# An order by hand for the first loads of a fused gated-convolution layer: SP's transfers and VectorE's instructions kept in plan order from the second to the twelfth pass

## Chip, cores and metric

One core of one Trainium2 chip. The metric is the time of one execution in microseconds (us). TensorE (PE in the profile) multiplies, VectorE (DVE) and ScalarE (ACT) do the elementwise work, GpSimd (POOL) a little of it, and SyncE (SP) issues nearly all transfers between HBM and the core's own memory, which 16 DMA engines carry out. Each engine works through its own instructions in a fixed order, and waits at an instruction whose inputs are not there yet.

## What is computed

One layer of a decoder trunk, for one sequence of 256 tokens with 2048 features, all in float32:

```python
h = rmsnorm(x, norm_g)
mod = einsum('bd,df->bf', silu(c), ada_w) + ada_b      # ada_w: 2048 x 6144
shift, scale, gate = split(mod, 3)
h = h * (1 + scale) + shift
b_gate, c_gate, v, g = split(h @ sc_w_in, 4)           # sc_w_in: 2048 x 16384
u = causal_depthwise_conv(c_gate * v, conv_w)          # width 3
y = (b_gate * u * silu(g)) @ sc_w_out                  # sc_w_out: 4096 x 2048
out = rmsnorm(x + gate * y, final_g)
```

## The kernel before

**Products.** Features lie on the 128 partitions, so the 2048 input features are 16 blocks k. A float32 product is made of three faster ones: a number is split into a high part (hi, a cast on ScalarE, line 356) and a low part (lo, the difference, on VectorE, line 361), and TensorE multiplies hi by hi, hi by lo and lo by hi (line 496). The tokens are split in the same way into hT. So each load of weights (raw_s, line 540) goes through three engines: SP's transfer, ScalarE's cast, VectorE's subtraction; then TensorE uses it. A load of 512 KB holds 8 blocks of 128 x 128, which are 24 matmuls of 256 columns.

**Why there are passes.** The block k of the tokens can only be used once shift and scale of these features are known, and these come from ada_w, 32 MB of which are read by the same DMA engines. The first two blocks are made ready in a written-out beginning. The other fourteen follow two at a time: a group of two blocks is read in eight pieces (`ada_piece`, line 454), each of two transfers of 256 KB (line 464) and two sums on VectorE (`ada_sums`, lines 476 and 478). After the eighth piece `ada_done` turns the sums on TensorE and finishes the two token blocks. Meanwhile TensorE works with the blocks that are there: the first 16 of 32 column tiles are 16 pairs (ch, q) of a chunk and a quarter, and a pass (`part`, line 522) multiplies one pair with the blocks k0 to k1. ScalarE or VectorE (`keep`, line 514) keeps the sum in acc for later passes.

**The plan.** `plan()` (line 52) simulates loads and engines with fixed costs and returns the order of passes and ada pieces. Its first steps, numbered from 0 (a pass is named with its blocks; n:m means k from n to m):

```
0 pass 0:2   1 pass 0:2   2 pass 0:2   3 ada 2   4 pass 0:2   5 ada 2   6 pass 0:2   7 pass 0:2
8 ada 2   9 pass 0:2   10 ada 2   11 pass 0:2   12 ada 2   13 pass 0:2   14 ada 2   15 pass 0:2
16 pass 0:2   17 ada 2   18 pass 0:2   19 ada 2   20 pass 0:2   21 ada 4   22 pass 0:4   23 ada 4
24 pass 0:4   25 ada 4   26 ada 4   27 pass 0:4   28 ada 4   ...
```

Step 0 is the first pass, whose weights the written-out beginning has loaded; steps 1, 2, 4, 6, 7, 9, 11, 13, 15, 16 and 18 are the second to the twelfth. Each loads 512 KB; step 22 is the first that loads 1024 KB. Steps 3 to 19 that say "ada 2" are the eight pieces for the blocks 2 and 3.

**Who sets the order on an engine.** The loop at line 575 traces the steps in plan order, but the framework's scheduler then orders each engine's instructions itself, by a priority (the order of tracing) and by when its own simulation has them ready. The kernel bends this in four ways: `in_order()` (line 166) chains all that is traced in it, engine by engine, and is used for the beginning (closed at line 434) and the end; `behind(last)` (line 179) puts instructions behind named ones of the same engine; `later(n)` (line 189) lowers the priority, and the ada sums are traced with `later(300)`; `tc.issue_after` does the same as `behind`. Such links cost no semaphore: they only fix an order. In `part`, high parts stand behind the copy that keeps an earlier pass (`kept`, line 545), and the low parts of the fourth and the fifth pass behind the last sum of the first and the second piece (`added`, line 547).

**Buffers.** raw, hi and lo have three tiles each, of 1024 KB. Two loads of 512 KB share one tile (`places`, line 369). Step 7's load goes to the tile that held the first pass's weights, step 11's to that of steps 1 and 2, step 22's to that of steps 11 and 13. The transfers of ada pieces have four tiles (at).

Of the kernel before, what the change touches and what calls it, by code (L numbers as in the profile page):

```python
# [51 lines left out]
def plan():  # L52

    steps, ready = [], [0.0] * ADA[0]
    done = {}
    pieces = [(sum(ADA[:g]), nk, i) for g, nk in enumerate(ADA) if g for i in range(4 * nk)]
    load, pe, dve, act = 0.0, 4.0, 0.0, 0.0  # L60
    burst = SLOT // P

    def ada():
        nonlocal load, dve
        k0, nk, i = pieces.pop(0)
        steps.append(("ada", k0, nk, i))
        load = max(load, dve - AAHEAD) + ALOAD
        dve = max(dve, load + 2.0) + VPIECE
        if i == 4 * nk - 1:
            ready.extend([dve + ALAG] * nk)  # L70

    def products(n, need):

        nonlocal load, pe, dve, act
        load = max(load, pe - WAHEAD)
        pe = max(pe, need, load + min(n, burst) * LOAD + WLAG) + n * PRODUCTS
        load += n * LOAD
        act = max(act, load + 2.0) + n * SBLOCK
        dve = max(dve, load + 2.0) + n * VBLOCK

    def fill():

        while pieces and max(load, dve - AAHEAD) + ALOAD + burst * LOAD + WLAG < pe:
            ada()

    order = [(ch, q) for ch in range(NCH) for q in QUARTERS]
    new = list(order)
    while new or any(k < KT for k in done.values()):
        fill()
        hi = sum(r <= pe for r in ready)  # L90
        if new:
            p = new.pop(0)
            done[p] = 0
        else:
            old = [p for p in order if done[p] < KT]
            p = old[0] if hi == KT else min(old, key=lambda p: done[p])
            while hi == done[p]:
                while len(ready) == hi:
                    ada()
                pe = max(pe, ready[hi])  # L100
                hi = sum(r <= pe for r in ready)
        products((hi - done[p]) * CT, ready[hi - 1])
        seed = done[p] > 0 and act < dve
        if done[p] == 0:
            act += SCOPY
        elif seed:
            act += SSEED
        else:
            dve += VSUM
        steps.append(("mm", *p, done[p], hi, seed))  # L110
        done[p] = hi
    while pieces:
        ada()
    return steps
# [3 lines left out]
def short_conv_layer(ctx: ExitStack, tc: tile.TileContext, x, c, norm_g, ada_w, ada_b, w_in, conv_w, w_out, final_g, out):  # L118
    nc = tc.nc
# [25 lines left out]
    def w_tile(kind, name, dtype=F32, i=None):  # L145

        if i is None:
            i = nth[kind] % 3
            nth[kind] += 1
        return wpool.tile([P, SLOT], dtype, tag=f"{kind}{i}", name=name, bufs=1)  # L150
# [12 lines left out]
    after = mybir.DependencyInfo(mybir.DependencyClass.NoSync, mybir.DependencyReason.DATA)  # L163

    @contextmanager
    def in_order():

        traced = nc.cur_bb.bb.instructions
        n = len(traced)
        yield  # L170
        last = {}
        for ins in list(traced[n:]):
            if ins.engine in last:
                tc.add_manual_dep(ins, last[ins.engine], after, reason="in order")
            last[ins.engine] = ins.name
        ended.update(last)

    @contextmanager
    def behind(last):

        traced = nc.cur_bb.bb.instructions
        n = len(traced)
        yield
        for ins in list(traced[n:]):
            if ins.engine in last:
                tc.add_manual_dep(ins, last[ins.engine], after, reason="behind")
# [13 lines left out]
    ended = {}  # L200
# [4 lines left out]
    def rows_tile(name):  # L205
        return const.tile([96, P], F32, tag="rows", name=name)
# [20 lines left out]
    for n, (j, kk) in enumerate(((0, 4), (4, 4), (8, 4), (12, 2), (14, 1), (15, 1))):  # L227
        at = w_tile(("lo", "hi")[n % 2], "at0")[:, : kk * 2 * NK0 * P]
        at = at.rearrange("p (k s f) -> p k s f", k=kk, s=2)
# [124 lines left out]
    def split_hi(raw, n, hi=None):  # L354
        hi = hi_tile() if hi is None else hi
        nc.scalar.copy(hi[:, :n], raw[:, :n])  # L356
        return hi

    def split_lo(raw, n, hi, lo_tag="lo", lo=None):
        lo = lo_tile(lo_tag) if lo is None else lo  # L360
        last_low[0] = nc.vector.tensor_tensor(  # L361
            out=lo[:, :n], in0=raw[:, :n], in1=hi[:, :n].bitcast(F32), op=ALU.subtract
        )
        return hi, lo
# [4 lines left out]
    def places(n):  # L369

        if n <= HALF and other_half[0]:
            tiles, other_half[0] = other_half[0], None
            return [b[:, HALF:SLOT] for b in tiles]
        tiles = raw_tile("raw_s"), hi_tile(), lo_tile()
        other_half[0] = tiles if n <= HALF else None
        return tiles
# [23 lines left out]
    for k in range(KT):  # L400
        c_k = silu_c[:, k : k + 1]
        at, gv = first_ada[k], gv0
        if k in ON_PE:
# [7 lines left out]
            at, gv = at[:, 1], gv0[:, 1]  # L411
# [59 lines left out]
    def ada_sums(j, kk, at4, gv):  # L471
        for i in range(kk):
            c_k = silu_c[:, j + i : j + i + 1]
            if j + i == 0:
                with behind(ended):
                    nc.vector.tensor_scalar_mul(gv, at4[:, i], c_k)
            else:
                nc.vector.scalar_tensor_tensor(out=gv, in0=at4[:, i], scalar=c_k, in1=gv, op0=ALU.mult, op1=ALU.add)  # L478
        added.append({ins.engine: ins.name for ins in nc.cur_bb.bb.instructions[-1:]})

    def ada_done(k0, nk, gv):

# [19 lines left out]
    def chunk_products(bank, hi, lo, o0, k, k0, k1, seed=False, late=False, parts=(0, 1, 2)):  # L502


        begins = k == k0 and not seed
        terms = [(m, i) for i in (0, 2, 1) for m in range(CT)] if late else [(m, i) for m in range(CT) for i in parts]
        for m, i in terms:
            o = slice(o0 + m * P, o0 + (m + 1) * P)
            product(bank[:, m, :], hi[:, o], lo[:, o], k, i, begins and i == 0, m % 2 == 0, 2 in parts and k == k1 - 1 and (m, i) == terms[-1])

    last_mm = [None]
    kept, added = [], []

    def keep(ch, q, k0, bank, seed=False):
        if k0 == 0 or seed:
# [6 lines left out]
    def part(ch, q, k0, k1, seed):  # L522


        col = q * E + ch * CT * P
        step = SLOT // (CT * P)
        first = k0
        bank = psum.tile([P, CT, T], F32, tag="mm", name="mm_s")
        if seed:
            nc.scalar.copy(bank, acc[ch, q])  # L530
        if pieces0:
            for k in range(NK0):
                chunk_products(bank, *pieces0[k], 0, k, k0, k1, late=True)
            pieces0.clear()
            k0 = NK0
        for s0 in range(k0, k1, step):
            sk = min(step, k1 - s0)
            n = sk * CT * P
            raw, hi, lo = places(n)
            nc.sync.dma_start(  # L540
                raw[:, :n].rearrange("p (k f) -> p k f", k=sk),
                w_in[0, s0 * P : (s0 + sk) * P, col : col + CT * P].rearrange("(k p) f -> p k f", p=P),
            )
            at = len(acc) if k0 == 0 else KT
            with behind(ended if at < 3 else kept[at - 3] if at < 9 else {}):
                split_hi(raw, n, hi)
            with behind(ended if at < 3 else added[at - 3] if at < 5 else {}):
                split_lo(raw, n, hi, lo=lo)
            for parts in ((0, 1), (2,)) if 0 < len(acc) < 3 else ((0, 1, 2),):
                for i in range(sk):  # L550
                    chunk_products(bank, hi, lo, i * CT * P, s0 + i, k0, k1, seed, parts=parts)
        if len(acc) == 1:
            with behind(ended):
                keep_x(3, tp_3)
        keep(ch, q, first, bank, seed)
        kept.append({ins.engine: ins.name for ins in nc.cur_bb.bb.instructions[-1:]})
# [14 lines left out]
            split_y(ys[-1], vq)  # L571

    LATER = (10, 14)
    whole = [0] * NCH
    for kind, *step in plan():
        if kind == "ada":
            ada_piece(*step)
        else:
            ch, k1 = step[0], step[3]
            part(*step)  # L580
            if step[2] == 0 and len(acc) in LATER:
                with tc.issue_after(last_mm[0].ins), behind(ended):
                    if len(acc) == LATER[0]:
                        rows2 = rows_tile("rows2")
                        nc.gpsimd.dma_start(rows2[:, :], conv_w.rearrange("w (k p) -> (w k) p", p=P))
                    else:
                        turn(rows2, 0, 96, cw)
            whole[ch] += k1 == KT
            if k1 == KT and whole[ch] == 4:
                mixed(ch)  # L590
# [354 lines left out]
```

## Time and profile before

| what | value |
|---|---|
| median of 3 runs | 903.0 us (902.49 to 903.24) |
| the profiled execution: time | 903.37 us |
| the profiled execution: span from first to last instruction | 901.6 us |
| ScalarE busy | 484.9 us, 54% |
| weights and ada transfers (queue q1) | 226.52 MB, 76.7% of the DMA engines' time |
| mean granted TensorE clock | 0.997 |

How to read the rows of the timeline that follow: start in us, duration in us, engine and line, operation, the tile written <- the tiles read, shape, xN for N instructions in a row that were merged, and in brackets the idle time of that engine just before and what ended it. PEld are TensorE's weight loads, which overlap its matmuls; SPq is SP issuing a transfer, and its duration is the issue, not the transfer. Rows of waits read: total us, times, longest us. Rows of windows read: window, length, then busy us (and instructions) of PE, PEld, DVE, ACT and POOL, then clock, DMA share and GB/s. Rows of DMA issues end with KB each and the median us from issue to landing.

### The profile page before, as it was taken

How to read it: one execution, taken by the hardware profiler on the slowest of the kernel's cores; microseconds unless marked ns; L12 is line 12 of the kernel's file. 1: busy time of each engine (PE TensorE's matmuls, PEld its weight loads, DVE VectorE, ACT ScalarE, POOL GpSimd, SP SyncE). 2: the span in 40 equal slices, each digit the busy share in tenths (PEclk: the TensorE clock that was granted, in tenths of full speed). 3: DMA queues.
4: the chain of work that ended last, by engine and by line, in shares of the span. 5: the costliest groups of instructions: out<-in, count | busy, mean ns of one | idle time of the engine just before them, and what ended most of it. 6: DMA issues, size and time to landing. Idle time of an engine off the chain costs nothing.

```text
span 901.6 us, 16416 instructions
## 1 busy us (share of the span) xinstructions
PE 887.4 (98%) x6997; PEld 850.6 (94%) x6997; DVE 675.3 (75%) x665; ACT 484.9 (54%) x429; POOL 84.8 (9%) x96
## 2 busy tenths in 40 slices
PE   7999999999999999999999999999999999999996
PEld 4899999999999999999999999999999988888885
DVE  5889989888888867765775678565555568879886
ACT  6768866665548856644443434444434445554543
POOL 0000000000000042024224302420000000000000
PEclk9999999999999999999999999999999999999998
DMA  9999999999998588687978898866666476673662
GB/s 307 365 369 368 368 315 348 356 369 352 351 326 289 165 277 250 192 257 229 295 227 247 256 289 269 240 198 197 201 193 188 141 284 222 199 275 123 203 234 94
DMA packets 159610, 235.01 MB, mean 261 GB/s; under 512 B 6900, under 2 KB 105284, under 8 KB 159152
## 3 DMA queue, kind: packets, MB, share of 16 engines
q1 hardware_dynamic: 156368, 226.52, 76.7%
q0 software_dynamic: 3040, 7.39, 2.8%
q8 instruction: 55, 0.90, 0.4%
q14 instruction: 19, 0.16, 0.1%
q10 hardware_dynamic: 128, 0.04, 0.0%
HBM read 224.49 MB, written 2.10 MB: 251 GB/s over the span
## 4 chain that ended last, share of the span: by engine, by line
PE 95%; DMA 3%; SPq 0%; ACT 0%; DVE 0%; issue 0%; ACTq 0%; DVEq 0%
PE mm_b L496 39%; PE mm_s L496 37%; PE mm_w L738 7%; PE mm_o L738 7%; PE mm L738 4%; DMA at<-in_ada_w_dram 2%; DMA x<-in_x_dram 1%; PE tp_g L486 0%; DVE lo L361 0%; SPq L464 0%; ACT hi L356 0%; ACT acc L518 0%; SPq L540 0%; SPq L218 0%; ACT big L852 0%
## 5 line engine op out<-in xcount | busy, mean ns | idle before, releaser
L496 PE MATMUL mm_s<-hT,hi 128*128 128x256 f32 x2048 | 348.4, 277 | 1.1 <-ACT hT L330 1.1
L496 PE MATMUL mm_b<-hT,hi 128*128 128x256 f32 x2048 | 348.2, 276 | 0.0
L496 PEld LDWEIGHTS mm_s<-hT,hi 128*128 128x128 f32 x2048 | 307.2, 188 | 1.3 <-ACT hT L330 1.3
L496 PEld LDWEIGHTS mm_b<-hT,hi 128*128 128x128 f32 x2048 | 308.2, 188 | 0.0
L496 PE MATMUL mm_b<-hT,lo 128*128 128x256 f32 x1024 | 282.8, 276 | 0.0
L496 PE MATMUL mm_s<-hT,lo 128*128 128x256 f32 x1024 | 280.2, 277 | 0.8 <-DVE lo L361 0.8
L356 ACT CAST hi<-raw 128x2048 fp32r<-128x2048 f32 (+1 forms) x66 | 123.7, 1875 | 193.5 <-PE mm_b L496 156.7
L361 DVE TENSOR_TENSOR lo<-raw,hi 128x2048 fp32r<-128x2048 f32 (+1 forms) x66 | 150.4, 2280 | 99.9 <-ACT hi L356 99.3
L496 PEld LDWEIGHTS mm_b<-hT,lo 128*128 128x128 f32 x1024 | 192.2, 188 | 0.0
L496 PEld LDWEIGHTS mm_s<-hT,lo 128*128 128x128 f32 x1024 | 190.7, 188 | 1.2 <-DVE lo L361 1.2
L361 DVE TENSOR_TENSOR lo<-raw_s,hi 128x2048 fp32r<-128x2048 f32 (+1 forms) x80 | 149.5, 1877 | 35.1 <-ACT hi L356 34.6
L356 ACT CAST hi<-raw_s 128x2048 fp32r<-128x2048 f32 (+1 forms) x80 | 124.2, 1558 | 58.2 <-PE mm_s L496 47.2
L478 DVE SCALAR_TENSOR_TENSOR gv<-at,silu_c,gv 128x512 f32<-128x512 f32 x105 | 78.5, 748 | 7.6 <-DMA at<-in_ada_w_dram 5.9
L518 ACT COPY acc<-mm_s 128x1024 f32<-128x1024 f32 x54 | 54.7, 1013 | 39.4 <-PE mm_s L496 39.2
L361 DVE TENSOR_TENSOR lo<-raw_o,hi 128x2048 fp32r<-128x2048 f32 x22 | 50.4, 2290 | 23.4 <-ACT hi L356 23.4
L356 ACT CAST hi<-raw_o 128x2048 fp32r<-128x2048 f32 x22 | 42.0, 1908 | 46.4 <-PE mm_w L738 12.6
L738 PE MATMUL mm_w<-hi,y 128*128 128x512 f32 x184 | 58.8, 389 | 0.0
L634 POOL TENSOR_TENSOR gacc<-gacc,z 128x512 f32<-128x512 f32 x28 | 44.7, 1597 | 116.2 <-DMA z<-gacc 116.2
L738 PE MATMUL mm_o<-hi,y 128*128 128x512 f32 x176 | 55.3, 389 | 0.0
L628 DVE SCALAR_TENSOR_TENSOR gacc<-at_g,silu_c,gacc 128x512 f32<-128x512 f32 x60 | 45.8, 764 | 8.2 <-DMA at_g<-in_ada_w_dram 7.2
L632 POOL DMA_DIRECT2D z<-gacc x28 | 15.6, 556 | 330.5 <-DVE acc L569 283.9
L738 PEld LDWEIGHTS mm_w<-hi,y 128*128 128x128 f32 x184 | 34.5, 188 | 7.2
(154 smaller groups left out, 689.4 us busy)
## 6 DMA issues: line engine op xcount, KB each, us to landing
raw<-in_sc_w_in_dram SPq DMA_DIRECT2D x64, 1024.0 KB, 5.8
raw_s<-in_sc_w_in_dram SPq DMA_DIRECT2D x47, 1024.0 KB, 8.3
raw_o<-in_sc_w_out_dram SPq DMA_DIRECT2D x32, 1024.0 KB, 5.3
at<-in_ada_w_dram SPq DMA_DIRECT2D x126, 256.0 KB, 7.9
raw_s<-in_sc_w_in_dram SPq DMA_DIRECT2D x33, 512.0 KB, 7.2
at_g<-in_ada_w_dram SPq DMA_DIRECT2D x32, 512.0 KB, 8.1
x<-in_x_dram SPq DMA_DIRECT2D x4, 512.0 KB, 6.3
big<-in_x_dram SPq DMA_DIRECT2D x2, 1024.0 KB, 8.2
```

The lines of the kernel that those rows point to most:

```text
L356: nc.scalar.copy(hi[:, :n], raw[:, :n])
L361: last_low[0] = nc.vector.tensor_tensor(out=lo[:, :n], in0=raw[:, :n], in1=hi[:, :n].bitcast(F32), op=ALU.subtract)
L478: nc.vector.scalar_tensor_tensor(out=gv, in0=at4[:, i], scalar=c_k, in1=gv, op0=ALU.mult, op1=ALU.add)
L496: mm = last_mm[0] = nc.tensor.matmul(dst, w, h[k], start=begins and left, stop=ends, skip_group_check=True)
L518: nc.scalar.copy(acc[ch, q], bank)
L628: nc.vector.scalar_tensor_tensor(out=ga, in0=at3[:, i, :], scalar=s, in1=ga, op0=ALU.mult, op1=ALU.add)
L632: nc.gpsimd.dma_start(turned[0 : P - away], ga[away:P])
L634: nc.gpsimd.tensor_tensor(out=ga, in0=ga, in1=turned, op=ALU.add)
L738: nc.tensor.matmul(dst, y[a], b, start=opens and i == 0, stop=ends and i == 2, skip_group_check=True)
```

## The change

`in_order` takes a set of engines, and the loop opens it at step 1 for SP and VectorE and closes it ahead of step 19. The list `added` and what used it go. ScalarE and TensorE are left to the scheduler as before, as is all from step 19 on.

```diff
     @contextmanager
-    def in_order():
+    def in_order(engines=None):
...
         for ins in list(traced[n:]):
+            if engines is not None and ins.engine not in engines:
+                continue
             if ins.engine in last:
                 tc.add_manual_dep(ins, last[ins.engine], after, reason="in order")
             last[ins.engine] = ins.name
-        ended.update(last)
+        if engines is None:
+            ended.update(last)
...
-        added.append({ins.engine: ins.name for ins in nc.cur_bb.bb.instructions[-1:]})
...
-    kept, added = [], []
+    kept = []
...
-            with behind(ended if at < 3 else added[at - 3] if at < 5 else {}):
+            with behind(ended if at < 3 else {}):
                 split_lo(raw, n, hi, lo=lo)
...
+    PLANNED = 19
     whole = [0] * NCH
-    for kind, *step in plan():
+    planned = ExitStack()
+    for n, (kind, *step) in enumerate(plan()):
+        if n == 1:
+            planned.enter_context(in_order((mybir.EngineType.SP, nc.vector.engine)))
+        elif n == PLANNED:
+            planned.close()
         if kind == "ada":
             ada_piece(*step)
```

The instructions themselves are the same in number, shape and kind. In the chain on VectorE stand, in this order, the low parts of steps 1 and 2, the two sums of piece 3, the low part of step 4, the sums of piece 5, the low parts of steps 6 and 7, the sums of piece 8, and so on to the low part of step 18; on SP the loads in the same order.

## Prediction

> **What bounds the kernel now.** I read the busy shares of the page first, then the waits of TensorE, then the timelines of weight loads, SP, VectorE and ScalarE around the change.
>
> ```profile
> span 901.6 us, 16416 instructions
> ...
> PE 887.4 (98%) x6997; PEld 850.6 (94%) x6997; DVE 675.3 (75%) x665; ACT 484.9 (54%) x429; POOL 84.8 (9%) x96
> ```
>
> TensorE is busy for 98% of the span. A busy share alone does not say that matmuls follow each other without holes, so the waits of TensorE over the whole run come next, and one window of full work.
>
> ```profile
> PE mm_s L496 <- ACT hT L330: 1.1, 1, 1.1
> PE mm_s L496 <- DVE lo L361: 0.8, 2, 0.5
> ```
>
> ```profile
> 50.00:60.00 10.00, 10.00 (x91) 10.00 (x90) 8.59 (x12) 7.56 (x8) 0.00 (x0) 1.00 1.06 373
> ```
>
> Once the main matmuls (mm_s) have begun, TensorE waits three times: once for its first tokens, ahead of everything that the change touches, and twice for a low part (lo, line 361) that VectorE had not finished. From 50 to 60 us it is busy for 10.00 of 10 us. So the change can win back at most those two holes. Their size is best read from the weight loads, which start at even steps when nothing is late:
>
> ```profile
> 33.22 0.30 PEld L496 LDWEIGHTS mm_s<-hT,hi 128*128 128x128 f32 x2
> 33.98 0.19 PEld L496 LDWEIGHTS mm_s<-hT,lo 128*128 128x128 f32 x1 [0.46 <-DVE lo L361]
> ...
> 39.22 0.30 PEld L496 LDWEIGHTS mm_s<-hT,hi 128*128 128x128 f32 x2
> 40.24 0.19 PEld L496 LDWEIGHTS mm_s<-hT,lo 128*128 128x128 f32 x1 [0.73 <-DVE lo L361]
> ...
> 62.25 0.30 PEld L496 LDWEIGHTS mm_s<-hT,hi 128*128 128x128 f32 x2
> 62.48 0.19 PEld L496 LDWEIGHTS mm_s<-hT,lo 128*128 128x128 f32 x1
> ```
>
> The last pair is the undisturbed rhythm: two loads take 62.48 - 62.25 = 0.23 us, so one step is 0.115 us and a pass of 24 matmuls 2.76 us. In the first pair the same two loads and the hole take 33.98 - 33.22 = 0.76 us, a loss of 0.53; in the second 40.24 - 39.22 = 1.02, a loss of 0.79. Together **1.32 us**: 0.15% of the span. The first hole is at the start of plan step 4, the second at the start of step 7 (24 matmuls a pass, counted from the first).
>
> **The change part by part.** What SP issues now, in order:
>
> ```profile
> 24.43 0.72 SPq L540 DMA_DIRECT2D raw_s<-in_sc_w_in_dram  x1
> 25.31 3.60 SPq L464 DMA_DIRECT2D at<-in_ada_w_dram  x4
> 30.50 3.33 SPq L540 DMA_DIRECT2D raw_s<-in_sc_w_in_dram  x4
> 34.26 2.88 SPq L464 DMA_DIRECT2D at<-in_ada_w_dram  x4
> 37.87 1.68 SPq L540 DMA_DIRECT2D raw_s<-in_sc_w_in_dram  x2
> 40.58 3.16 SPq L464 DMA_DIRECT2D at<-in_ada_w_dram  x4
> 44.19 2.09 SPq L540 DMA_DIRECT2D raw_s<-in_sc_w_in_dram  x2
> 46.38 1.96 SPq L464 DMA_DIRECT2D at<-in_ada_w_dram  x2
> 48.78 0.37 SPq L540 DMA_DIRECT2D raw_s<-in_sc_w_in_dram  x1
> ```
>
> Read beside the plan, 24.43 is the load of step 6. The plan goes on with 7, 8 (ada), 9, 10 (ada), 11, 12 (ada), 13; SP instead issues both ada pieces, 8 and 10 (four transfers), and then 7, 9, 11 and 13 in one row. That is the only large departure: 12 and 14 precede 15 and 16 here, and 17 and 19 precede 18 and 20, where the plan has 17, 18, 19, 20.
>
> *SP.* No instruction is added; transfers change places. Step 7's 512 KB go ahead of four transfers of 256 KB, step 9's ahead of two. What a place is worth comes from the rate:
>
> ```profile
> DMA packets 8918, 12.09 MB, mean 366 GB/s; under 512 B 519, under 2 KB 5586, under 8 KB 8913
> ```
>
> ```profile
> raw_s<-in_sc_w_in_dram SPq DMA_DIRECT2D x1, 512.0 KB, 7.3
> ```
>
> The first row is the stretch from 25 to 58 us, in which the DMA engines are full in every slice: 366 GB/s make 1.43 us of 512 KB and 0.72 of 256 KB. The second is step 7's load, issued at 30.50, landed at 37.8. Behind step 6, which landed just ahead of 33.48 (below), it would land at 33.45 + 1.43 = 34.9. Pieces 8 and 10 get later by 1.4 to 2.9 us, and from step 15 on nothing has moved. Step 7's load must wait until the first pass's tile is free, whose low parts VectorE does ahead of those of steps 1 and 2, and behind it on SP wait pieces 8 onwards. A transfer lands 7.3 us behind its issue, which is at least five transfers' worth, so a short hold of SP leaves the engines work; without that cover it would cost what the DMA engines stand still.
>
> *VectorE and ScalarE.*
>
> ```profile
> 32.04 0.75 DVE L478 SCALAR_TENSOR_TENSOR gv<-at,silu_c,gv 128x512 f32<-128x512 f32 x1 [1.44 <-DMA at<-in_ada_w_dram]
> 32.71 1.22 DVE L361 TENSOR_TENSOR lo<-raw_s,hi 128x1024 fp32r<-128x1024 f32 x1
> ...
> 34.56 1.23 DVE L361 TENSOR_TENSOR lo<-raw_s,hi 128x1024 fp32r<-128x1024 f32 x1
> ...
> 60.08 2.29 DVE L361 TENSOR_TENSOR lo<-raw_s,hi 128x2048 fp32r<-128x2048 f32 x1
> ```
>
> ```profile
> 30.49 1.05 ACT L356 CAST hi<-raw_s 128x1024 fp32r<-128x1024 f32 x1
> ...
> 33.48 1.05 ACT L356 CAST hi<-raw_s 128x1024 fp32r<-128x1024 f32 x1 [1.03 <-DMA raw_s<-in_sc_w_in_dram]
> 34.43 1.01 ACT L518 COPY acc<-mm_s 128x1024 f32<-128x1024 f32 x1
> 36.80 1.02 ACT L518 COPY acc<-mm_s 128x1024 f32<-128x1024 f32 x1 [1.37 <-PE mm_s L496]
> 37.88 1.05 ACT L356 CAST hi<-raw_s 128x1024 fp32r<-128x1024 f32 x1
> ...
> 57.96 1.92 ACT L356 CAST hi<-raw_s 128x2048 fp32r<-128x2048 f32 x1 [0.29 <-DMA raw_s<-in_sc_w_in_dram]
> ```
>
> First hole: VectorE sits 1.44 us idle before a sum of piece 5, while the high part of step 4 ended at 30.49 + 1.05 = 31.54. In plan order step 4's low part comes ahead of both sums: 31.58 + 1.22 = 32.8, where TensorE asks for it at 33.22 + 0.23 = 33.45. The hole of 0.53 closes with 0.65 to spare. The two sums of piece 5 then end near 34.4; step 6's low part keeps its 34.56, because its data landed then.
>
> Second hole: TensorE reaches step 7's low part at 39.22 + 0.23 - 0.53 = 38.9. Step 7's data are there at 34.9, ScalarE is free after the copy of 34.43 at 35.4, so its high part ends at 36.5 and its low part at 37.7: 1.2 us early. If ScalarE kept its present order (step 4's copy, now 36.80 - 0.53 = 36.3, first), the high part would end at 38.4 and the low part at 39.6, and 0.7 of the 0.79 would stay. Both ends are kept; I take the first, since the data now come well before that copy. The wait lists for the high parts (line 545) allow it.
>
> Behind that, VectorE must keep up: 11 low parts of 1.22 and 7 pieces of two sums of 0.75 are 13.4 + 10.5 = 23.9 us against TensorE's 11 x 2.76 = 30.4. A low part queued behind a sum cannot be held long by that sum's transfer, since SP now issues in the same order and the sum's data land before those of the low part. So both holes go: minus 1.32, by the end of step 20.
>
> *What is late next.* Step 22, the first with 1024 KB. Its transfer:
>
> ```profile
> raw_s<-in_sc_w_in_dram SPq DMA_DIRECT2D x1, 1024.0 KB, 9.1
> ```
>
> Issued at 48.78, it landed at 57.9; ScalarE was waiting for it (57.96 above) and ended at 59.88, VectorE ended the low part at 60.08 + 2.29 = 62.37, TensorE used it at 62.48. There is 0.1 us of slack. Ahead of this load stand exactly the same bytes in the new order (passes up to 20, pieces up to 21), and the DMA engines are never empty, so it lands at 57.9 again. TensorE, 1.32 earlier, wants the low part at 61.16. The earliest is 57.96 + 1.92 + 0.04 + 2.29 = 62.21, the latest with the present order 62.37; TensorE starts about 0.04 later. So **1.1 to 1.25 us come back as a new wait at step 22**, and 0.07 to 0.23 remain; I take 0.2, as the step in which VectorE was 0.2 late (59.88 to 60.08) is behind a sum that may move. Later steps have the same DMA rate behind them, so I expect no second gain. The sum against the profiled execution (903.37 us, with 901.6 of span): 903.37 - 0.2 = 903.2; its distance to the median of 903.0 is spread between runs, so on the median **902.8 us**.
>
> The rate is the premise of this. [...]
>
> **The rivals.** A: *the whole gain stays*, 903.0 - 1.32 = 901.7. For it: from step 19 on the scheduler places transfers anew, and if piece 21 (1.43 us of transfer) fell behind step 22's load, this would land at 56.5 and hold TensorE by nothing. Against: piece 21 stands ahead of step 22 in the plan and in the trace. [...] B: *the holes do not close*, because another wait (ScalarE's order, a buffer) keeps the low parts where they are: 903.0, or 902.4 with the first hole alone if step 22 did not take it. C, *slower*: the schedule behind step 18 is made anew and a piece that now follows step 22's load (its slack is 0.1) goes ahead of it. Each piece is 1.43 us of transfer, or 1.5 us of sums if it is put ahead of the low part on VectorE. One piece: 903.0 + 1.43 - 0.1 = 904.3; two: 905.8. It decides as soon as step 22's low part ends after 62.4. For it: VectorE already put one sum of the next piece in front of that low part. Against: up to step 18 the new order leaves ada work no later than before from step 15 on, so there is no reason to hurry pieces.
>
> **How the numbers follow.** A measurement of this kernel can tell about 0.2%, 1.8 us, from no change. Forecast (0.5 us either side of 902.8) 0.46; A 0.12; B 0.09; C with one piece 0.09, with two or more 0.21; and 0.03 for a gain over 1.8 us, which the two holes cannot pay. So faster 0.03, same 0.46 + 0.12 + 0.09 + 0.09 = 0.76, slower 0.21. The range goes from A (901.7, rounded to 901.6) to two pieces, 905.8; three or more, and 0.03 below, stay outside.
>
> **What would show it.** Right: no wait of TensorE for a low part before 50 us, step 7's load right behind step 6's on SP, and one new wait of about 1.1 us near 61 to 62 us that ends with VectorE's first low part of 128x2048. Wrong in the first half: a hole still stands between 33 and 41 us. Wrong in the second: step 22's 1024 KB land clearly before or after 57.9, or TensorE waits at several places after 62 us.

## The result and the profile after

| kernel | median | lowest to highest | executions |
|---|---|---|---|
| before | 903.06 us | 902.49 to 903.47 | 8 |
| after | 905.26 us | 904.17 to 906.84 | 8 |

The ratio is 1.0026, with a 95% interval of 1.0015 to 1.0037: the change made the kernel **slower** by 2.2 us, where the forecast was a gain of 0.2 us. Two executions among those of the experiments took far longer than the rest (1287 us, the profiled one of e6, and 2685.5 us, one of e4) and are used neither as times nor as profiles.

The executions of the changed kernel fall into two groups of four: 904.17 to 904.66 us at a mean granted clock of 0.997 to 0.998, and 905.87 to 906.84 us at 0.996. The profile is one of the second group: 906.84 us, with a span of 905.1.

The page first, then TensorE's waits over the whole run (total us, times, longest us).

```profile
span 905.1 us, 16415 instructions
...
PE 889.2 (98%) x6997; PEld 852.1 (94%) x6997; DVE 673.8 (74%) x665; ACT 484.2 (54%) x429; POOL 89.5 (10%) x96
```

```profile
PE mm_s L498 <- DVE lo L364: 1.9, 1, 1.9
PE mm_s L498 <- ACT hT L333: 1.1, 1, 1.1
PE mm L746 <- ACT hi L774: 0.8, 1, 0.8
```

The two waits for a low part are gone, and one longer wait stands in their place. TensorE's busy time grew from 887.4 to 889.2 us although it does the same 6997 matmuls: some of them ran slower. The last row is a wait near the end of the kernel, where a load of output weights sometimes lands late; it is also 0.8 us in the profile of e4 below, 0.2 to 0.4 in those of e1 to e3 and absent from those of the kernel before, e8 and e9, so it varies between executions and is not counted to the change.

The weight loads of TensorE show where the wait is. They begin with the first two loads of step 4, of step 7 and of step 22.

```profile
33.04 0.30 PEld L498 LDWEIGHTS mm_s<-hT,hi 128*128 128x128 f32 x2
33.26 0.19 PEld L498 LDWEIGHTS mm_s<-hT,lo 128*128 128x128 f32 x1
...
38.48 0.30 PEld L498 LDWEIGHTS mm_s<-hT,hi 128*128 128x128 f32 x2
38.70 0.19 PEld L498 LDWEIGHTS mm_s<-hT,lo 128*128 128x128 f32 x1
...
60.72 0.30 PEld L498 LDWEIGHTS mm_s<-hT,hi 128*128 128x128 f32 x2
63.08 0.19 PEld L498 LDWEIGHTS mm_s<-hT,lo 128*128 128x128 f32 x1 [2.05 <-DVE lo L364]
```

At steps 4 and 7 the pair now takes 0.22 us, the undisturbed rhythm: both holes are closed. At step 22 it takes 63.08 - 60.72 = 2.36 us, a loss of 2.13 against 0.23. The windows behind it (busy us of PE, PEld, DVE, ACT, POOL, then the granted clock) show a second loss:

```profile
62.00:63.00 1.00, 0.00 (x0) 0.00 (x0) 1.00 (x2) 1.00 (x2) 0.00 (x0) 1.00 1.05 381
63.00:64.00 1.00, 0.92 (x7) 0.93 (x8) 1.00 (x4) 1.00 (x1) 0.00 (x0) 1.00 1.05 366
64.00:65.00 1.00, 1.00 (x8) 1.00 (x7) 1.00 (x4) 0.66 (x1) 0.00 (x0) 0.57 1.11 362
65.00:66.00 1.00, 1.00 (x6) 1.00 (x6) 1.00 (x3) 0.33 (x1) 0.00 (x0) 0.50 1.09 348
66.00:67.00 1.00, 1.00 (x6) 1.00 (x6) 1.00 (x1) 1.00 (x1) 0.00 (x0) 0.50 1.09 366
67.00:68.00 1.00, 1.00 (x8) 1.00 (x7) 1.00 (x2) 0.57 (x1) 0.00 (x0) 0.72 1.05 377
68.00:69.00 1.00, 1.00 (x11) 1.00 (x10) 0.53 (x1) 0.00 (x0) 0.00 (x0) 1.00 1.06 384
```

TensorE is 100% busy from 64 to 68 us, yet from 65 to 67 a window counts 6 matmuls instead of 11 (a count takes in those that only reach into the window): the granted clock is halved. The four clocks lack 0.43 + 0.50 + 0.50 + 0.28 = 1.71 us of work; at half clock that is 3.42 us of time. A busy share can't show this, the column of the clock can.

So for the profiled executions (906.84 against 903.37, 3.47 more): two holes closed, -1.32; the wait at step 22, +2.13; the half clock, +1.71; the wait near the end, +0.8; together 3.32. Without half clock and late wait, the change costs 0.8.

Where the wait at step 22 comes from is read from SP, ScalarE and VectorE. SP first:

```profile
23.79 2.95 SPq L542 DMA_DIRECT2D raw_s<-in_sc_w_in_dram  x2
26.78 2.09 SPq L467 DMA_DIRECT2D at<-in_ada_w_dram  x2
28.92 0.47 SPq L542 DMA_DIRECT2D raw_s<-in_sc_w_in_dram  x1
...
41.72 1.80 SPq L542 DMA_DIRECT2D raw_s<-in_sc_w_in_dram  x2
43.82 3.78 SPq L467 DMA_DIRECT2D at<-in_ada_w_dram  x4
48.03 0.37 SPq L542 DMA_DIRECT2D raw_s<-in_sc_w_in_dram  x1
```

Steps 6 and 7 are now one row: step 7's load follows step 6's directly, as the plan has it. But look at the end of the chain. The loads of steps 18 and 20 are also one row now, ahead of the four transfers of pieces 19 and 21. In the kernel before, piece 19 was in the row of four at 40.58, ahead of both. The chain puts piece 17 and step 18 in plan order and ends ahead of step 19; the scheduler, free again, took step 20 first. So the eighth and last piece of the group is fetched two loads later. What it holds up is seen on ScalarE and VectorE:

```profile
57.83 1.02 ACT L520 COPY acc<-mm_s 128x1024 f32<-128x1024 f32 x1 [1.70 <-PE mm_s L498]
58.74 1.91 ACT L359 CAST hi<-raw_s 128x2048 fp32r<-128x2048 f32 x1
```

```profile
53.06 0.75 DVE L481 SCALAR_TENSOR_TENSOR gv<-at,silu_c,gv 128x512 f32<-128x512 f32 x1 [0.17 <-DMA at<-in_ada_w_dram]
54.38 1.23 DVE L364 TENSOR_TENSOR lo<-raw_s,hi 128x1024 fp32r<-128x1024 f32 x1 [0.57 <-ACT hi L359]
55.53 0.75 DVE L481 SCALAR_TENSOR_TENSOR gv<-at,silu_c,gv 128x512 f32<-128x512 f32 x1
...
59.40 0.69 DVE L489 TENSOR_REDUCE gs<-tp_g 128x4 f32<-128x512 f32 x1 [1.94 <-PE tp_g L488]
60.01 0.74 DVE L481 SCALAR_TENSOR_TENSOR gv<-at,silu_c,gv 128x512 f32<-128x512 f32 x1
60.67 0.15 DVE L329 TENSOR_TENSOR mod<-gs,vec 128x4 f32<-128x4 f32 x1
60.74 2.28 DVE L364 TENSOR_TENSOR lo<-raw_s,hi 128x2048 fp32r<-128x2048 f32 x1
```

Two orders changed on engines that the change doesn't touch. *ScalarE:* the copy of step 18's result (57.83) now stands ahead of step 22's wide high part. It waits 1.70 us for TensorE to finish that step, while the data of the high part have been there since 48.03 + 9.1 = 57.1 (the row below is that load's issue, with KB and us to landing). Before, the high part went first, at 57.96.

```profile
raw_s<-in_sc_w_in_dram SPq DMA_DIRECT2D x1, 1024.0 KB, 9.1
```

*TensorE:* the four transposes of the group's sums (tp_g, from `ada_done`) moved from 56.58, one matmul into step 18, to 58.76, ten matmuls into step 20. VectorE has done the sums by 56.3, but its queue stands still for 1.94 us at the reduction that reads those transposes, and the sum, the modulation and the wide low part are queued behind it. The low part ends at 63.02; TensorE, with its two holes closed, wanted it at 60.72 + 0.23 = 60.95. The transposes before and after:

```profile
56.58 0.60 PE L486 MATMUL tp_g<-ident,gv 128*128 128x128 f32 x4
```

```profile
58.76 0.60 PE L488 MATMUL tp_g<-ident,gv 128*128 128x128 f32 x4
```

### The profile page after: what moved, and what is told of

It reads as the page before. It is cut to its first block, busy times and chain, and to the rows that moved or that the text cites. A ratio compares the mean times of both kernels' runs of the same rounds, so it can differ in the third digit from the quotient of the medians.

```text
span 905.1 us, 16415 instructions
## 1 busy us (share of the span) xinstructions
PE 889.2 (98%) x6997; PEld 852.1 (94%) x6997; DVE 673.8 (74%) x665; ACT 484.2 (54%) x429; POOL 89.5 (10%) x96
## 4 chain that ended last, share of the span: by engine, by line
PE 94%; DMA 3%; DVE 1%; ACT 1%; issue 0%; SPq 0%; ACTq 0%; DVEq 0%
PE mm_s L498 39%; PE mm_b L498 38%; PE mm_w L746 7%; PE mm_o L746 6%; PE mm L746 4%; DMA at<-in_ada_w_dram 1%; DMA x<-in_x_dram 1%; DMA raw_o<-in_sc_w_out_dram 1%; PE tp_g L488 0%; ACT hi L359 0%; DVE lo L364 0%; DVE gv L418 0%; DVE lo L777 0%; ACT hi L774 0%; DVE sums_o L769 0%
## 5 line engine op out<-in xcount | busy, mean ns | idle before, releaser
L364 DVE TENSOR_TENSOR lo<-raw,hi 128x2048 fp32r<-128x2048 f32 (+1 forms) x66 | 153.5, 2327 | 98.9 <-ACT hi L359 98.7
L642 POOL TENSOR_TENSOR gacc<-gacc,z 128x512 f32<-128x512 f32 x28 | 49.4, 1766 | 119.7 <-DMA z<-gacc 119.7
```

Source lines behind the costliest of these rows:

```text
L364: last_low[0] = nc.vector.tensor_tensor(out=lo[:, :n], in0=raw[:, :n], in1=hi[:, :n].bitcast(F32), op=ALU.subtract)
L642: nc.gpsimd.tensor_tensor(out=ga, in0=ga, in1=turned, op=ALU.add)
```

## Experiments

Two theories were set against each other at first: that one of the two moved orders makes the wait (ScalarE's or TensorE's), or that each alone is enough. Then came the half clock, and the question which part of the change does it.

### e1: ScalarE's order put back

```diff
             with behind(ended if at < 3 else kept[at - 3] if at < 9 else {}):
                 split_hi(raw, n, hi)
+            if (ch, q, k0) == (3, 2, 0):
+                made = [i for i in nc.cur_bb.bb.instructions[-1:]]
+                tc.add_manual_dep(copies[2, 0], made[-1].name, after, ...)
```

`copies` keeps the copy of each pass; step 22 is (3, 2, 0), step 18 is (2, 0). So only the copy goes behind the wide high part.

> Only ScalarE's order differs from the changed kernel: the high part of step 22 stands ahead of the copy that keeps step 18. Theory 1 (two queues hold step 22's low part equally long: ScalarE's high part until 60.65, VectorE's sums and the bias addition behind TensorE's transposes until 60.82): the high part ends at about 59.1 instead of 60.65, the low part still starts at about 60.8, TensorE's hole stays at 2.0 us, the time stays at 904.2 to 906.8. Rival 1 (ScalarE's order alone is the cause): the low part starts at about 59.2, the hole shrinks to 0.4 us, the time falls to about 903.

Measured: 904.64 us (904.01 to 907.20), ratio 1.0020 (1.0011 to 1.0029). ScalarE, then VectorE:

```profile
57.57 1.91 ACT L359 CAST hi<-raw_s 128x2048 fp32r<-128x2048 f32 x1 [1.43 <-DMA raw_s<-in_sc_w_in_dram]
```

```profile
59.42 0.69 DVE L489 TENSOR_REDUCE gs<-tp_g 128x4 f32<-128x512 f32 x1 [1.95 <-PE tp_g L488]
...
60.76 2.28 DVE L364 TENSOR_TENSOR lo<-raw_s,hi 128x2048 fp32r<-128x2048 f32 x1
```

The high part is 1.2 us earlier, and the low part not at all: VectorE is still held by the transposes. ScalarE's order alone isn't the cause.

### e2: the transposes put back

```diff
+            turned_g[k0] = nc.tensor.transpose(...).ins           # in ada_done
...
+                    with behind({turned_g[2].engine: turned_g[2].name} if (ch, q, k0) == (3, 1, 0) else {}):
                         chunk_products(bank, hi, lo, i * CT * P, s0 + i, k0, k1, seed, parts=parts)
```

Step 20 is (3, 1, 0); its products now stand behind the group's transposes, which start at 57.66. That is not quite the old place, one matmul into step 18: there the sums, done at 56.3, would come too late now.

> The transposes of the finished sums of blocks 2 and 3 stand ahead of step 20's matmuls on TensorE instead of among them; ScalarE's order around step 22 is that of the changed kernel. Theory 1: VectorE is free for the low part of step 22 by about 59.8, but its high part still ends at 60.65, so the low part starts at about 60.7, the hole stays at 2.0 us and the time at 904.2 to 906.8. Rival 2 (VectorE's wait for the transposes alone is the cause): the low part starts at about 59.8, the hole is 1.0 us, the time about 903.5 to 904.

Measured: 905.07 us (904.02 to 906.15), ratio 1.0018 (1.0009 to 1.0027). VectorE:

```profile
58.30 0.69 DVE L490 TENSOR_REDUCE gs<-tp_g 128x4 f32<-128x512 f32 x1 [0.82 <-PE tp_g L489]
...
60.71 2.29 DVE L364 TENSOR_TENSOR lo<-raw_s,hi 128x2048 fp32r<-128x2048 f32 x1 [0.86 <-ACT hi L359]
```

VectorE is through with its small work at 59.8, 0.86 us early, and now waits for the high part instead. The low part starts at 60.71 once more. The two delays lie side by side and are equally long, so taking away either one gives nothing.

### e3: both put back

Both edits together.

> Both edits together: high part of step 22 ahead of the copy, transposes ahead of step 20's matmuls. Theory 1: the low part starts at about 59.8 (behind one sum of piece 23), the hole is about 1.0 us; the time is 903.06 - 1.32 + 1.0 + 0.3 for tighter later steps, 903.0 to 903.6, and the half clock behind the hole is rarer or gone. Rivals 1 and 2, each for itself, would have shown their gain in the run with one edit already and nothing more here.

Measured: 903.13 us (902.64 to 906.18), ratio 1.0002 (0.9993 to 1.0011): level with the kernel before. VectorE, TensorE's loads and a window:

```profile
59.98 2.29 DVE L364 TENSOR_TENSOR lo<-raw_s,hi 128x2048 fp32r<-128x2048 f32 x1
```

```profile
62.31 0.19 PEld L499 LDWEIGHTS mm_s<-hT,lo 128*128 128x128 f32 x1 [1.05 <-DVE lo L364]
```

```profile
64.00:65.00 1.00, 1.00 (x11) 1.00 (x10) 1.00 (x3) 0.10 (x1) 0.00 (x0) 1.00 1.06 358
```

The low part is 0.76 us earlier, the wait is 1.05 us (a loss of 1.1 by the pairs of loads, the size that the prediction gave to it), and the clock stays at 1.00. With both orders put back, the forecast's time comes out within 0.4 us (902.8 against 903.13). Two of the eleven executions stand apart, 904.75 and 906.18 us; neither was traced. Against e1, e2 and the changed kernel this is 1.5 to 2.1 us less, although the wait is only 1.0 us shorter: the half clock has gone with it.

### e4 and e8: the wide low parts ahead of the sums

e4 has both edits of e3 and also puts the sums of piece 23 behind step 22's low part; e8 does the same with the sums that follow step 24's.

```diff
+            if (ch, q, k0) == (3, 2, 0):              # e8: in ((3, 2, 0), (3, 3, 0))
+                wide_low.update({ins.engine: ins.name for ins in nc.cur_bb.bb.instructions[-1:]})
...
+                with behind(wide_low if wide_low and len(acc) == 14 else {}):    # e8: in (14, 15)
                     nc.vector.scalar_tensor_tensor(out=gv, ...)
```

> Both edits, and the sums of piece 23 behind step 22's low part. Theory 1: the high part ends at about 59.1, the low part follows at 59.2 and ends at 61.4 to 61.5; TensorE asks for it at 61.07: a hole of 0.4 us, no half clock, and 902.1 to 902.9: both holes of before gone, most of the new one too. If the load's landing alone (57.15) were the bound, it could not get better than this.

> As the run with both edits and the low part of step 22 first, and in the same way the sums of pieces 23 to 25 behind the low part of step 24, which there ended 0.2 to 0.4 us too late. Theory 1: step 24's low part starts at 64.0 instead of 64.7 and ends at 66.3, before TensorE asks for it at 66.8; of the holes only the 0.45 us at step 22 is left, so 903.2 - 1.32 + 0.45 = about 902.3 us, 902.0 to 902.9. If later steps take the gain back, 902.8 as in that run or more.

Measured: e4 902.81 us (902.21 to 903.42), ratio 0.9994 (0.9985 to 1.0003); e8 903.24 us (902.21 to 904.50), ratio 0.9999 (0.9990 to 1.0007). TensorE's loads in e8:

```profile
61.52 0.19 PEld L501 LDWEIGHTS mm_s<-hT,lo 128*128 128x128 f32 x1 [0.39 <-DVE lo L364]
```

The wait falls to 0.39 us (0.38 in e4). e4's time lies in the expected range; e8's median lies above the 902.0 to 902.9 that was expected. Neither version can be told from the kernel before: e8's profile, at 902.50 us, has little left to win in this stretch, but its executions spread over 2.3 us, five of them near 902.4 and five near 903.5. What separates these two groups wasn't found.

### e5 and e6: which part of the change does it

e5 chains SP alone and keeps the list `added`; e6 chains VectorE alone, without `added`.

```diff
-            planned.enter_context(in_order((mybir.EngineType.SP, nc.vector.engine)))
+            planned.enter_context(in_order((mybir.EngineType.SP,)))        # e6: (nc.vector.engine,)
```

> Only SP's transfers are kept in plan order; VectorE is left to the scheduler as before, with the list added still there. Theory 1 (the order of SP's transfers alone makes the scheduler lay out all that follows as in the changed kernel): both early holes of TensorE are gone, the hole of 2.0 us at step 22 is there, 904.0 to 906.8 us. Rival 3 (VectorE's chain closes the holes or opens the new one): holes at 33 or 39 us remain, or the hole near 61 us is missing; 902.5 to 903.5 us.

> Only VectorE's instructions are kept in plan order; SP is left to the scheduler, so step 7's load goes behind four transfers of pieces 8 and 10 again. Theory 1: the first hole (step 4) closes, the second stays at 0.8 us or grows, since step 7's data come at 37.8 us as before, and VectorE's sums of later pieces now wait behind the low parts; the order behind step 18 is a third one, with its own holes near 60 to 70 us. 903 to 906 us. Rival 3: both holes close as in the changed kernel.

Measured: e5 906.18 us (904.69 to 906.49), ratio 1.0029 (1.0018 to 1.0039). e6 905.56 us (905.22 to 906.37), ratio 1.0027 (1.0017 to 1.0037). e10 is e6 once more, for its profile:

> VectorE's chain alone once more, for a profile in an undisturbed execution. SP keeps the old order, so step 7's load is issued behind the transfers of pieces 8 and 10 and lands near 37.8 us. If VectorE's chain alone costs what the timed runs said (905.6, at a clock of 0.997 to 0.999, so with no half clock): the holes are spread over steps 4 to 20, since the sums of piece 8 now stand behind the low part of step 7; the hole at step 22 is below 2 us. If it costs it at one place, TensorE has one wait of over 2 us between 33 and 63 us.

Measured: 905.67 us. TensorE's load at step 22 in e5:

```profile
63.42 0.19 PEld L499 LDWEIGHTS mm_s<-hT,lo 128*128 128x128 f32 x1 [2.05 <-DVE lo L364]
```

and its three waits for a low part in e10, with the instruction on VectorE that ends the first of them:

```profile
39.91 0.19 PEld L498 LDWEIGHTS mm_s<-hT,lo 128*128 128x128 f32 x1 [0.96 <-DVE lo L364]
...
63.34 0.19 PEld L498 LDWEIGHTS mm_s<-hT,lo 128*128 128x128 f32 x1 [1.08 <-DVE lo L364]
...
67.46 0.19 PEld L498 LDWEIGHTS mm_s<-hT,lo 128*128 128x128 f32 x1 [1.19 <-DVE lo L364]
```

```profile
38.63 1.23 DVE L364 TENSOR_TENSOR lo<-raw_s,hi 128x1024 fp32r<-128x1024 f32 x1 [3.18 <-ACT hi L359]
```

SP's chain alone makes the same wait of 2.05 us, so VectorE's chain isn't needed for the loss of the full change. Nor is it needed for most of the gain: in e5 the pairs of loads at steps 4 and 7 take 0.34 and 0.23 us, so 0.11 us is left of the two holes. VectorE's chain alone costs as much in another way. With SP's old order step 7's data come late, and VectorE, no longer free to do sums meanwhile, stands idle for 3.18 us: that makes the first wait. The other two end with the low parts of steps 22 and 24. They come 23 us and more later, and no wait for a low part lies between, so that they follow from the first isn't shown. Ahead of step 22's low part VectorE waits 1.10 us for a transfer and 0.69 us for the group's transposes. The three waits are 0.96 + 1.08 + 1.19 = 3.2 us, where the same column has 0.46 + 0.73 = 1.2 before. The clock is 0.997 or more in all nine of these executions, with waits of up to 1.2 us. The holes are spread, as was expected, but two of the three lie at steps 22 and 24, where steps 4 to 20 had been named.

### e7: the wait made longer

Step 22's low part is followed by forming its first half again, with the same result, and the sums of piece 23 go behind it as in e4.

```diff
                 split_lo(raw, n, hi, lo=lo)
+            if (ch, q, k0) == (3, 2, 0):
+                with behind({ins.engine: ins.name for ins in nc.cur_bb.bb.instructions[-1:]}):
+                    split_lo(raw, n // 2, hi, lo=lo)
```

> The changed kernel, and VectorE forms the first half of step 22's low part a second time (the same values), which makes TensorE wait about 2 us longer: a hole of about 4.0 us instead of 2.0. Theory on the clock (a hole of 2.0 us halves the granted clock for 3.4 us in about half of the executions, one of 1.1 us in none seen so far): with 4.0 us the half clock follows in every execution, and costs 1.7 us of matmuls each time; 906.3 + 2.0 = 908 to 909 us, and all executions in one group. Rival (the half clock comes by chance, whatever the hole): the executions fall in two groups 1.8 us apart again.

Measured: 909.00 us (907.02, 908.69, 909.31, 909.33), ratio 1.0067 (1.0051 to 1.0082). The profiled one is the 907.02:

```profile
64.88 0.29 PEld L500 LDWEIGHTS mm_s<-hT,lo 128*128 128x128 f32 x1 [3.79 <-DVE lo L364]
```

```profile
65.00:66.00 1.00, 1.00 (x5) 1.00 (x6) 1.00 (x3) 0.26 (x1) 0.00 (x0) 0.50 1.15 345
...
68.00:69.00 1.00, 1.00 (x10) 1.00 (x9) 1.00 (x2) 0.00 (x0) 0.00 (x0) 0.91 1.06 402
```

The wait grew by 1.74 us. The median lies 2.7 us above the mean of the changed kernel's slower group (906.31), so the wait stands on the path that ends the kernel. The profiled execution lies only 0.2 above the profiled 906.84, but that one has the 0.8 us wait near the end and this one doesn't. The three other executions take 1.7 to 2.3 us more than the profiled one, so the expectation that all would lie in one group isn't met; two of them have a clock of 0.994, which would fit a second halved stretch, but neither was traced, and the third has 0.997. That stays open.

### e9: the wait filled with matmuls

```diff
+            if (ch, q, k0) == (3, 2, 0):
+                for _ in range(16):
+                    nc.tensor.matmul(bank[:, 0, :], hi[:, :P], hh_[0], start=True, stop=True, skip_group_check=True)
             for parts in ((0, 1), (2,)) if 0 < len(acc) < 3 else ((0, 1, 2),):
```

> The changed kernel with 16 extra matmuls ahead of step 22's products: they multiply the first block's high part by the first token block into the same bank, which the real products then begin anew, so the output is unchanged. They need only step 22's high part, so TensorE works on them from about 60.9 to 62.7 us (16 x 0.115 = 1.84), while the low part is still being formed; the wait for the low part falls from 2.0 to about 0.2 us, and nothing else starts earlier. Theory (the half clock is TensorE's answer to its standing idle for 2.0 us, and not to the order of the transfers): no half clock behind step 22 in any execution, clock 0.997 or more in all of them, time that of the undisturbed group of the changed kernel, 904.2 to 904.7, median 904.4. Rival (the half clock belongs to something else in that stretch, such as the transfers or the first pass of new blocks): about half of the executions still have a clock of 0.996 or less and lie at 905.9 to 906.9.

Measured: 904.18 us (903.95 to 904.63), ratio 1.0011 (1.0002 to 1.0020); the clock is 0.998 or 0.999 in all eleven executions. TensorE's loads, then a window:

```profile
60.72 1.89 PEld L553 LDWEIGHTS mm_s<-hT,hi 128*128 128x128 f32 x16
62.53 0.30 PEld L498 LDWEIGHTS mm_s<-hT,hi 128*128 128x128 f32 x2
63.07 0.19 PEld L498 LDWEIGHTS mm_s<-hT,lo 128*128 128x128 f32 x1 [0.24 <-DVE lo L364]
```

```profile
64.00:65.00 1.00, 1.00 (x11) 1.00 (x10) 1.00 (x4) 0.66 (x1) 0.00 (x0) 1.00 1.08 355
```

The low part comes no sooner (63.07 against 63.08), so the wait costs what it did. But TensorE no longer stands idle, and the half clock is gone from every execution. All of them lie in the range of the faster group of the changed kernel or up to 0.2 us below it, and their median is 1.1 us below that of the changed kernel. The medians leave 0.94 us over the kernel before (903.24 beside e9), near the 0.8 that the sum of the two profiles gives without half clock and late wait. Sixteen matmuls whose results are thrown away made the changed kernel faster, which speaks for the half clock being the answer to the idle time, and not to the transfers or to the new blocks. One reservation: e9 was executed on another chip than e1 and e2, and e5, which show the half clock on two chips; so that it would have come on e9's chip at all is not shown by itself. The places of the falls, at the end of this document, speak for the idle time too.

### The half clock, counted over all kernels

A stretch of 3.42 us at half clock takes 1.71/903 = 0.0019 from the mean clock, so a mean of 0.996 or less marks such an execution. The mark can miss one: executions without the stretch lie between 0.997 and 0.999, so one with it can come out at 0.997. The profiles agree with the mark: those of the changed kernel, e1 and e2 (0.995 to 0.996) show the stretch, those of e3, e4, e5, e8 and e9 (0.998 or more) don't.

| idle time at step 22 | kernels | executions at 0.996 or less |
|---|---|---|
| 3.8 us | e7 | 3 of 4 |
| 2.0 us | after, e1, e2, e5 | 17 of 36 |
| 0.4 to 1.1 us | e3, e4, e8 | 0 of 32 |
| 1.1 and 1.2 us (and 1.0 at step 7) | e6, e10 | 0 of 9 |
| 0.2 us, filled | e9 | 0 of 11 |

By their times, two executions at 0.997 could be ones that the mark misses: e3's 904.75 us and e7's 909.33.

## Why the prediction was wrong

**What bounds the kernel, and the two holes.** Right. Both holes closed: the pairs of loads at steps 4 and 7 take 0.22 us.

**SP.** Right up to step 18. Step 7's load landed at 34.44 (34.9 forecast) and its low part ended at 37.27 (37.7). Of the two ends that were kept for ScalarE's order there, the one taken was the right one. Wrong was the sentence that from step 15 on nothing moves: it was true of the bytes ahead of step 22's load, which landed at 57.15, 0.7 earlier than forecast. It wasn't true of piece 19, which moved from ahead of the loads of steps 18 and 20 to behind them. The rate under the sum held: 366 GB/s from 25 to 58 us before and 369 after.

**What is late next: the step that failed.** The prediction named the place (step 22), the instruction (the first low part of 128x2048) and the number of waits (one). It bounded the wait between 1.1 and 1.25 us, and took as the far end the present order of the queues. That wasn't the far end. The scheduler laid the queues of ScalarE and TensorE anew, although the diff names neither, and two delays of the same size arose side by side. The wait was 2.13 us. That SP's new order brings this about is shown by e5. That it is piece 19's later fetch in it is argued from the order of the queues: no run closed the chain one step later, behind step 19, to test it. e3 confirms the step under its own premise: with both orders put back the wait is 1.05.

**What the sum lacked.** The half clock. A wait was priced at its length. Somewhere between 1.2 us of idle time, which has no such stretch behind it by the mark (0 of 41 executions), and 2.0 us another 1.7 us come in about half of the executions (17 of 36). The holes of the kernel before (0.5 and 0.8 us) had shown nothing of it.

**The rivals.** C named the right mechanism in its first half, a schedule made anew behind step 18, and its times (904.3 and 905.8) lie near the two groups that came out, and the measured median lies inside the stated range only because of it. That nearness is chance, since its means were others: no piece went ahead of step 22's load, since that landed earlier and not later, and no additional sum is the price. It was priced by the transfers and sums of pieces, where the cost is the order on two other engines and the clock. A fell with the wait at step 22, B with the closed holes (its second time should have been 903.0 - 0.53 = 902.5, not 902.4).

**The forecast as a whole.** The sum was -1.32 + 1.1 = -0.2. Measured were -1.32 + 2.13 for all executions and +1.7 for about half of them: -1.32 + 2.13 + 0.85 = 1.7 of the 2.2 us. The rest, 0.5 us, is within what the wait near the end takes or leaves from one execution to the next; that this is its whole cause isn't shown.

## What to carry to other kernels

Fixing the order on one engine can change what the scheduler does on others, from the point where the fixed part ends: the two orders that cost the time here stood on engines that the diff doesn't name, so read the built order of every engine behind the fixed stretch, and keep the far end of a bound for an order that isn't there yet. When a late instruction has two inputs that come at the same time, putting right either of them alone brings nothing (e1, e2), and only both together tell the cause (e3). Work that a matmul engine does for nothing can be worth its place: where the wait of 2 us stayed, filling it spared the stretch at half clock behind it in all eleven executions (e9: a median of 904.18 us, against 905.26 for the changed kernel).

## What the runs showed of the hardware

In 17 of 36 executions, by the mean clock, TensorE's idle time of 2.0 us was followed by a stretch at half clock; in the profiles of the changed kernel, e1 and e2 it is a granted clock of 0.50 for 3.42 us. In the profile of the changed kernel the fall comes 1.06 us after TensorE has begun again: the window from 64 lacks 0.43, which is 0.86 us at half clock, so it fell at 64.14. Idle times up to 1.2 us have no such stretch behind them by the same mark (0 of 41), and e9 speaks for the idling as the cause.

Why only about half of the executions show it can be read from the places of the falls. The clock falls once more at the end of the kernel, when TensorE has finished. First the changed kernel, then e5:

```profile
900.00:901.00 1.00, 0.00 (x0) 0.00 (x0) 0.29 (x1) 0.47 (x1) 0.00 (x0) 0.70 0.52 203
```

```profile
899.00:900.00 1.00, 0.00 (x0) 0.00 (x0) 0.00 (x0) 0.00 (x0) 0.00 (x0) 0.56 1.09 389
```

The first row lacks 0.30, so the clock fell at 900.40. That is 836.26 us after 64.14. In the same profile windows of 0.01 us put the fall at 64.14 and the rise back to 1.00 at 67.55, so the stretch is 3.41 us long, and 836.26 is 245.2 times that: by this estimate 245 steps of 836.26/245 = 3.413 us lie between the two falls. The profiles of e1, e2 and e7 give the same 836.26 us (63.44 to 899.70, 64.06 to 900.32, 64.76 to 901.02), although their spans are 904.6, 904.4 and 905.2 us beside 905.1. So by these four profiles the falls stand on a grid with steps of 3.41 us, whose place differs from execution to execution. In the changed kernel, e1 and e2 the step ahead of the first fall holds the wait of 2.0 us whole (in the changed kernel, 61.03 to 63.08 within 60.73 to 64.14); in e7 that step is idle all through. e5's profile has the same wait and no half clock behind it: its fall at 899.12 puts a grid point at 899.12 - 836.26 = 62.86, and this cuts the wait (61.37 to 63.42) into 1.49 and 0.56 us. In all five profiles with a wait of 2.0 us or more, then, its place on the grid tells whether the half clock follows. As an estimate from these numbers, a wait of 2.05 us that begins anywhere lies whole within a step of 3.41 us in 1.36/3.41 = 40% of the cases; counted were 47%. How much idle time in one step is enough, between 1.49 and 2.0 us, wasn't tested, and executions without a profile can't be placed on the grid.
